# A squared-ReLU MLP on Trainium2: in the last quarter, two of the eight outputs over all tokens and six in two passes by token half

## The chip, the core and the metric

The kernel is one program on one core of a Trainium2 chip. The metric is the device time of one execution in microseconds (us), as a median over runs. The engines are called PE (TensorE, with PEld for its weight loads), DVE (VectorE), ACT (ScalarE), POOL (GpSimd) and SP (SyncE, which issues the loads). Each of them works through its own instructions in the order in which the program lists them, and waits where an operand or a buffer isn't ready.

## What is computed

Two layers run over 512 tokens, 256 of context and 256 latent, with 1024 features. Layer 0 mixes tokens by a convolution module, layer 1 by a bidirectional mLSTM, and each layer is followed by an MLP. What matters here is the end of layer 0 and the first product of layer 1:

```
h  = layer_norm(ALPHA * h + g2 * (square(relu(u @ w1)) @ w2))   # layer 0, latent and context rows
u' = h * (1 + scale) + shift                                    # modulation for layer 1
z  = u'[latent] @ up_z                                          # layer 1, latent rows only
xm = u' @ up_x                                                  # layer 1, all rows
```

The hidden width of the MLP is 4096. The layer norm goes over the 1024 features of a token, so it can be finished for a token only when all eight blocks of 128 features are there.

## The kernel before

**Layout.** Features lie on the 128 partitions and tokens on the free dimension: columns 0 to 255 are context (`LO`, s = 0), 256 to 511 latent (`HI`, s = 1). The residual stream is eight tiles x of 128x512. An fp32 product is made of three matmuls (`mm3`, lines 181, 184, 185): the weight is split into a rounded part wh and a rest wl, the activation likewise, and wh·hi, wh·lo and wl·hi are added in PSUM. For each weight block of 128x1024 `split_w` has ACT cast wh (line 150) and DVE subtract for wl (line 151). One output (128 features) over 1024 inputs takes 8 x 3 = 24 matmuls.

**The MLP.** `mlp` (line 1040) takes the hidden width in four quarters c. A quarter makes eight hidden tiles hid (`e1`) and then adds its share to the eight x tiles (`e2`, whose line 1071 is a DVE instruction per output and token half). For c < 3 the second product is a `gemm` over all 512 tokens. For c = 3 it is `gemm2` (line 284): pass 1 makes all eight outputs for the latent half, pass 2 all eight for the context half, each matmul 256 columns wide. The order of pass 2 is the list `AGAIN`, 4 5 6 7 0 1 2 3 (line 1109).

**Buffers.** Split weights go round a ring of four (`NW`); a slot comes free when its last matmul has read it. `gemm2` keeps outputs 0 to 3 in the ring over both passes, and 4 to 7 in tiles u (`keep`). Raw weights go round a ring of three, loaded by SP.

**The norm.** In the last quarter `feed0` (line 1111) hands each finished half tile to a `Norm` (line 487). With the fourth tile of a half it has a sum, whose mean is made on PE (line 507) and copied by ACT (508); with the fifth, all tiles so far are shifted on DVE (523), squared on ACT (525, 528), and sums and squares are collected on DVE (529, 531, 533). After the eighth, `finish` (line 536) takes PE matmuls (543), small DVE and ACT steps (545 to 553) and PE transposes (556). Then `u1_half` (line 1125) applies it, tile by tile: two DVE instructions (561, 562), two on ACT for hi and a full-precision copy S (584), one on DVE for lo (585).

**Order around the change.** The latent half is finished first, since `up_z` (line 1156) reads only latent columns. `feed0` advances `u1_half(1)` by two tiles at each output of pass 2, and `u1_half(0)` goes along with the outputs of `up_z`. `up_z` begins with three outputs side by side (`ko=3`). The order within an engine isn't written by hand: a scheduler lists each engine's instructions when the program is built.

Of the kernel before, what the change touches and what calls it, by code (L numbers as in the profile page):

```python
# [71 lines left out]
def hybrid_kernel(ctx: ExitStack, tc: tile.TileContext, xT, vecs_d, wdw_d, ada0_w, ada_w, wg_d, pw1a, pw1, pw2, w1_0, w2_0,  # L72
# [18 lines left out]
    def tmp(tag, dt=F32):  # L91
        return tp.tile([P, T], dt, tag=tag, name=nm(tag), bufs={"E": 4, "S": 2, "L": 2, "F": 1}[tag])
# [56 lines left out]
    def split(hi, lo, src):  # L149
        c = nc.scalar.copy(hi, src)  # L150
        lastsub[0] = nc.vector.tensor_tensor(lo, src, hi.bitcast(F32), op=ALU.subtract).ins  # L151
        return c.ins
# [68 lines left out]
    def gemm(*a, **k):  # L221
        for _ in gemm_steps(*a, **k):
            pass
# [60 lines left out]
    def gemm2(*a, **k):  # L284
        for _ in gemm2_steps(*a, **k):
            pass
# [180 lines left out]
    def comb(l, gname, bname, sc, sh, streams=(0, 1)):  # L467

        ca = con.tile([P, 2, DT], F32, name=nm("ca"))
        cb = con.tile([P, 2, DT], F32, name=nm("cb"))  # L470
        for s in streams:
            nc.vector.scalar_tensor_tensor(ca[:, s, :], ad(l, s, sc), 1.0, VA(gname), op0=ALU.add, op1=ALU.mult)
            nc.vector.scalar_tensor_tensor(cb[:, s, :], ad(l, s, sc), 1.0, VA(bname), op0=ALU.add, op1=ALU.mult)
            nc.vector.tensor_tensor(cb[:, s, :], cb[:, s, :], ad(l, s, sh), op=ALU.add)
        return ca, cb
# [8 lines left out]
    HALVES = [(0, LO), (1, HI)]  # L484


    class Norm:
# [22 lines left out]
        def feed(self, t):  # L510

            self.ts.append(t)
            if len(self.ts) <= 4:
                self.add(t)
                return
            if len(self.ts) == 5:
                self.mean()
            for x_ in self.ts[self.i:]:
                self.shift(x_)
# [520 lines left out]
    def mlp(w1, w2, uu, res, n, g2, feed, hmake, after, each1=None, each=None, keep=None, pre=None):  # L1040

        def part(c):
            hid = {}

            def e1(m, ps, s=None, sl=slice(0, n)):
                r, q = tmp("E")[:, :ps.shape[-1]], tmp("E")[:, :ps.shape[-1]]
                nc.scalar.activation(r, ps, AF.Relu)
                nc.vector.tensor_tensor(q, r, r, op=ALU.mult)
                if m not in hid:
                    if n == T:  # L1050
                        hid[m] = hmake(F32R), hmake(F32R)
                    else:
                        t = hmake(F32R)
                        hid[m] = t[:, :n], t[:, n:2 * n]
                split(hid[m][0][:, sl], hid[m][1][:, sl], q)
                if each1:
                    each1(c, m, s)

            groups = range(4 * c, 4 * c + 4)
            if keep and c == 0:  # L1060
                gemm2(w1, groups[:3], uu, HALVES, e1, keep, ko=3)
                gemm(w1, groups[3:], uu, n, lambda m, ps: e1(m + 6, ps))
            else:
                gemm(w1, groups, uu, n, e1, ko=0 if c else 3 + Z.pre4 if pre else 3, pre=pre if c == 0 else None)
            after(c)

            def e2(m, ps, s=None, sl=slice(0, n)):
                for s_, g, sl_ in g2:
                    if s is None or s == s_:
                        p_ = ps if s is not None else ps[:, sl_]  # L1070
                        nc.vector.scalar_tensor_tensor(res[m][:, sl_], p_, g[:, m:m + 1], res[m][:, sl_],
                                                       op0=ALU.mult, op1=ALU.add)
                if c == 3:
                    feed(m, s)
                if each:
                    each(c, m, s)

            hs = [hid[i] for i in range(8)]
            if keep and c == 3:
                gemm2(w2[c], range(4), hs, HALVES[::-1], e2, keep, again=AGAIN)  # L1080
            else:
                gemm(w2[c], range(4), hs, n, e2, ko=Z.kw2)

        for c in range(4):
            part(c)
# [9 lines left out]
    def each1(c, m, s):  # L1095
        if c == 0 and uside:
            for _ in range(Z.nu2):
                next(uside[0], None)
        if c in (1, 2) or (c == 3 and m < 2):
            ada_n1.step()  # L1100
# [5 lines left out]
    lns = norm_pair(maker(hp, "ln", 3))  # L1106
    cab1, u1, sides = [], {}, []

    AGAIN = [4, 5, 6, 7, 0, 1, 2, 3]

    def feed0(m, s):
        sl = HALVES[s][1]
        lns[s].feed(x[m][:, sl])
        if len(lns[s].ts) == DT:
            lns[s].finish()
            if not cab1:
                ada_n1.flush()
                cab1.extend(comb(1, "ln2_g0", "ln2_b0", "sc1", "sh1"))
            if s == 1:
                sides.append(u1_half(s))  # L1120
        if s == 0 and sides:
            for _ in range(2):
                next(sides[0], None)

    def u1_half(s):
        for i in range(DT):
            f = i if s else AGAIN[i]
            xn = lns[s].apply(i)
            if s:
                u1[f] = U(F32R), U(F32R)  # L1130
            affine_half(*[t[:, HALVES[s][1]] for t in u1[f]], xn, s, *cab1, f)
            yield

    mlp(w1_0, w2_0, uu, x, T, [(s, ad(0, s, "g2"), sl) for s, sl in HALVES], feed0, HD, after0, each1, each0, keep=U)


# [849 lines left out]
```

## Time and profile before

| | |
|---|---|
| median of 3 runs | 1671.9 us (1670.12 to 1672.25) |
| the profiled execution | 1670.06 us |
| its span, first to last instruction | 1668.3 us |
| PE busy | 1656.0 us, 8920 matmuls |
| DVE busy | 1030.2 us |
| ACT busy | 742.2 us |
| mean granted PE clock | 0.998 |

The profile is of one execution. A timeline row gives the start in us from the span's start, the duration, the engine, the line and the operation, then written and read tiles; idle time ahead of it stands in brackets with what ended it. Matmuls overlap in their pipeline, so the distance between two starts tells their cost, not the duration. The same holds in part for DVE and ACT: consecutive instructions start a little before the one ahead has ended. A row of the stages gives the length of a stretch, the busy time of each engine with its instructions, the granted clock, and the share and rate of the DMA engines.

### The profile page before, as it was taken

How to read it: one execution, taken by the hardware profiler on the slowest of the kernel's cores; microseconds unless marked ns; L12 is line 12 of the kernel's file. 1: busy time of each engine (PE TensorE's matmuls, PEld its weight loads, DVE VectorE, ACT ScalarE, POOL GpSimd, SP SyncE). 2: the span in 40 equal slices, each digit the busy share in tenths (PEclk: the TensorE clock that was granted, in tenths of full speed). 3: DMA queues.
4: the chain of work that ended last, by engine and by line, in shares of the span. 5: the costliest groups of instructions: out<-in, count | busy, mean ns of one | idle time of the engine just before them, and what ended most of it. 6: DMA issues, size and time to landing. Idle time of an engine off the chain costs nothing.

```text
span 1668.3 us, 22876 instructions
## 1 busy us (share of the span) xinstructions
PE 1656.0 (99%) x8920; PEld 1364.9 (82%) x8920; DVE 1030.2 (62%) x1857; ACT 742.2 (44%) x1196; POOL 14.3 (1%) x64
## 2 busy tenths in 40 slices
PE   9999999999999999999999999999999999999998
PEld 6665898888888998877788899888878888878887
DVE  6555895666635765761143663564389876786677
ACT  4313573232324476652243532442368654655453
POOL 0000000000000000000000000000000000000001
PEclk9999999999999999999999999999999999999999
DMA  9565223444324064556775743455375556675552
GB/s 359 201 216 208 85 75 114 151 145 136 136 101 152 10 233 160 185 194 251 266 259 174 259 171 120 143 198 175 130 246 190 192 213 213 253 274 190 179 186 92
DMA packets 73901, 301.63 MB, mean 181 GB/s; under 512 B 7518, under 2 KB 23682, under 8 KB 43968
## 3 DMA queue, kind: packets, MB, share of 16 engines
q1 hardware_dynamic: 56080, 285.44, 48.3%
q10 hardware_dynamic: 17712, 14.72, 2.6%
q8 instruction: 70, 1.15, 0.3%
q14 instruction: 39, 0.32, 0.1%
HBM read 284.37 MB, written 15.77 MB: 180 GB/s over the span
## 4 chain that ended last, share of the span: by engine, by line
PE 96%; DVE 2%; DMA 1%; issue 0%; ACT 0%; SPq 0%; ACTq 0%; DVEq 0%
PE mm L181 17%; PE mm L184 17%; PE mm L185 17%; PE mm L196 7%; PE mm L212 4%; PE mm L214 4%; PE mm L213 4%; PE mm L197 4%; PE cv L212 2%; PE cv L214 2%; PE cv L213 2%; PE fl L343 1%; PE ln L181 1%; PE cv L839 1%; PE ln L184 1%; PE ln L185 1%
## 5 line engine op out<-in xcount | busy, mean ns | idle before, releaser
L151 DVE TENSOR_TENSOR wl<-raw,wh 128x1024 fp32r<-128x1024 f32 x344 | 418.9, 1222 | 276.2 <-ACT wh L150 263.5
L150 ACT CAST wh<-raw 128x1024 fp32r<-128x1024 f32 x344 | 358.7, 1051 | 502.3 <-PE mm L184 278.3
L184 PE MATMUL mm<-u,wh 128*128 128x512 f32 (+1 forms) x808 | 291.6, 361 | 0.2 <-DVE u L594 0.2
L181 PE MATMUL mm<-u,wh 128*128 128x512 f32 (+1 forms) x680 | 243.6, 359 | 0.0
L185 PE MATMUL mm<-u,wl 128*128 128x512 f32 (+1 forms) x680 | 241.3, 355 | 0.0
L184 PEld LDWEIGHTS mm<-u,wh 128*128 128x128 f32 x808 | 152.6, 189 | 22.2 <-DVE u L594 0.5
L181 PEld LDWEIGHTS mm<-u,wh 128*128 128x128 f32 x680 | 128.4, 189 | 25.2 <-issue 5.9
L185 PEld LDWEIGHTS mm<-u,wl 128*128 128x128 f32 x680 | 128.4, 189 | 18.6 <-issue 0.8
L212 PE MATMUL mm<-wh,xl 128*128 128x512 f32 x256 | 101.0, 395 | 0.1
L181 PE MATMUL mm<-xm,wh 128*128 128x512 f32 x256 | 101.0, 394 | 0.0
L213 PE MATMUL mm<-wh,xl 128*128 128x512 f32 x256 | 100.0, 391 | 0.0
L185 PE MATMUL mm<-xm,wl 128*128 128x512 f32 x256 | 99.7, 390 | 0.0
L214 PE MATMUL mm<-wl,xl 128*128 128x512 f32 x256 | 99.2, 391 | 0.0
L181 PE MATMUL mm<-hid,wh 128*128 128x512 f32 (+1 forms) x256 | 93.3, 364 | 0.0
L185 PE MATMUL mm<-hid,wl 128*128 128x512 f32 (+1 forms) x256 | 92.8, 363 | 0.0
L184 PE MATMUL mm<-hid,wh 128*128 128x512 f32 (+1 forms) x256 | 92.8, 363 | 0.0
L196 PE MATMUL mm<-x,wh 128*128 128x512 f32 x232 | 81.1, 398 | 0.0
L426 DVE SCALAR_TENSOR_TENSOR S<-ar,cs,S 128x512 f32<-128x512 f32 x56 | 40.8, 749 | 59.4 <-DMA ar<-ada_w 59.2
L184 PE MATMUL mm<-qq,wh 128*128 128x272 f32 x256 | 73.9, 289 | 0.0
L181 PE MATMUL mm<-qq,wh 128*128 128x272 f32 x256 | 73.5, 288 | 0.0
L185 PE MATMUL mm<-qq,wl 128*128 128x272 f32 x256 | 73.5, 288 | 0.0
L196 PE MATMUL mm<-u,wh 128*128 128x512 f32 x192 | 68.7, 399 | 0.0
(535 smaller groups left out, 3253.2 us busy)
## 6 DMA issues: line engine op xcount, KB each, us to landing
raw<-w SPq DMA_DIRECT2D x64, 1024.0 KB, 4.8
raw<-wo SPq DMA_DIRECT2D x32, 1024.0 KB, 4.8
raw<-ada_w SPq DMA_DIRECT2D x22, 1024.0 KB, 6.5
ar<-ada_w SPq DMA_DIRECT2D x80, 256.0 KB, 3.7
raw<-wv SPq DMA_DIRECT2D x16, 1024.0 KB, 6.8
raw<-wqT SPq DMA_DIRECT2D x16, 1024.0 KB, 6.2
raw<-wq SPq DMA_DIRECT2D x16, 1024.0 KB, 4.9
raw<-wk SPq DMA_DIRECT2D x16, 1024.0 KB, 5.1
```

Of the source, the lines that this page charges most:

```text
L150: c = nc.scalar.copy(hi, src)
L151: lastsub[0] = nc.vector.tensor_tensor(lo, src, hi.bitcast(F32), op=ALU.subtract).ins
L181: a = nc.tensor.matmul(ps, wh, xh, start=start, stop=False)
L184: nc.tensor.matmul(ps, wh, xl, start=False, stop=False)
L185: lastmm[0] = nc.tensor.matmul(ps, wl, xh, start=False, stop=stop).ins
L196: todo = [lambda s_, e_: nc.tensor.matmul(ps, wh, r[0], start=s_, stop=e_), lambda s_, e_: nc.tensor.matmul(ps[:, :n], wl, r[0][:, :n], st ...
L197: lambda s_, e_: nc.tensor.matmul(ps[:, :n], wl, r[0][:, :n], start=s_, stop=e_)]
L212: nc.tensor.matmul(ps, xh, wh, start=start, stop=False)
L213: nc.tensor.matmul(ps, xl, wh, start=False, stop=False)
L214: nc.tensor.matmul(ps, xh, wl, start=False, stop=stop)
L343: a = mark_unit[0] = nc.tensor.matmul(ps[32 * j:32 * j + 32], cs[:, kt, 14 - 2 * v:46 - 2 * v], blocks[kt], start=first and kt < 4, stop=l ...
L426: nc.vector.scalar_tensor_tensor(a, w, c, a, op0=ALU.mult, op1=ALU.add)
```

## The change

For c = 3 the second product is now a `gemm` of the first group (outputs 0 and 1, all 512 tokens) and then a `gemm2` of the other three groups: six outputs for the latent half, then six for the context half, in the order 6 7 2 3 4 5. Outputs 0 and 1 feed the norms of both halves at once (`s is None`). `AGAIN` is now the order in which context tiles reach their norm, and is used by `u1_half(0)`.

```diff
             if keep and c == 3:
-                gemm2(w2[c], range(4), hs, HALVES[::-1], e2, keep, again=AGAIN)
+                gemm(w2[c], range(1), hs, n, e2)
+                gemm2(w2[c], range(1, 4), hs, HALVES[::-1], lambda m, *r: e2(m + 2, *r), keep, again=[4, 5, 0, 1, 2, 3])
             else:
                 gemm(w2[c], range(4), hs, n, e2, ko=Z.kw2)
...
-    AGAIN = [4, 5, 6, 7, 0, 1, 2, 3]
+    AGAIN = [0, 1, 6, 7, 2, 3, 4, 5]

     def feed0(m, s):
+        if s is None:
+            feed0(m, 1)
+            feed0(m, 0)
+            return
         sl = HALVES[s][1]
         lns[s].feed(x[m][:, sl])
```

Pass 2 ends with the four outputs whose weights lie in the ring, before and after. Lines of the changed kernel are one higher from line 1081 on and five higher from about line 1112 on; the helpers' lines are the same. The scheduler lists the instructions around the hand-over to `up_z` anew, at three places.

On PE, the end of pass 2 and the start of `up_z`. Before, these rows stand there (mm_5193 is the last output of pass 2, mm_5270 and mm_5275 are the first two of `up_z`; the u on the left of a pair are hi and lo of the latent u'):

```order
L185 MATMUL mm_5193<-hid_4569,wl_4672 128x256
L181 MATMUL mm_5270<-u_4941,wh_5266 128x256
L184 MATMUL mm_5270<-u_4942,wh_5266 128x256
L185 MATMUL mm_5270<-u_4941,wl_5267 128x256
L181 MATMUL mm_5275<-u_4941,wh_5271 128x256
L184 MATMUL mm_5275<-u_4942,wh_5271 128x256
L185 MATMUL mm_5275<-u_4941,wl_5272 128x256
```

Now it is these, with mm_5135 the last output of pass 2, and mm_5212, mm_5217, mm_5224 and cv_5316 the first four outputs of `up_z`:

```order
L185 MATMUL mm_5135<-hid_4569,wl_4761 128x256
L181 MATMUL mm_5212<-u_4937,wh_5208 128x256
L184 MATMUL mm_5212<-u_4938,wh_5208 128x256
L181 MATMUL mm_5217<-u_4937,wh_5213 128x256
L184 MATMUL mm_5217<-u_4938,wh_5213 128x256
L181 MATMUL cv_5316<-u_4937,wh_5297 128x256
L184 MATMUL cv_5316<-u_4938,wh_5297 128x256
L181 MATMUL mm_5224<-u_4937,wh_5220 128x256
L184 MATMUL mm_5224<-u_4938,wh_5220 128x256
L185 MATMUL mm_5212<-u_4937,wl_5209 128x256
```

The first wl is read by the ninth matmul of `up_z` where it was the third, and a matmul of the fourth output, with its wh, stands among the first eight.

On DVE, the last two outputs of pass 2 (lines 1071 of x_213 and x_259) and what stands around them. Before, the wl of the first `up_z` output (wl_5267) is some rows above this piece, and the last of `u1_half(1)` (line 585) above that:

```order
L1071 SCALAR_TENSOR_TENSOR x_213<-mm_5162,ada_97,x_213 128x256
L151 TENSOR_TENSOR wl_5272<-raw_5264,wh_5271 128x1024
L523 TENSOR_TENSOR x_213<-x_213,ln_2181 128x256
L151 TENSOR_TENSOR wl_5279<-raw_5276,wh_5278 128x1024
L529 TENSOR_TENSOR ln_2182<-ln_2182,L_5189 128x256
L533 TENSOR_TENSOR ln_2180<-ln_2180,x_213 128x256
L1071 SCALAR_TENSOR_TENSOR x_259<-mm_5193,ada_97,x_259 128x256
L151 TENSOR_TENSOR wl_5356<-raw_5276,wh_5355 128x1024
```

Now, with the last two outputs x_305 and x_351:

```order
L1071 SCALAR_TENSOR_TENSOR x_305<-mm_5104,ada_97,x_305 128x256
L562 TENSOR_TENSOR x_443<-x_443,ln_4889 128x256
L585 TENSOR_TENSOR u_5091<-S_5092,u_5090 128x256
L523 TENSOR_TENSOR x_305<-x_305,ln_2181 128x256
L1071 SCALAR_TENSOR_TENSOR x_351<-mm_5135,ada_97,x_351 128x256
L533 TENSOR_TENSOR ln_2180<-ln_2180,x_305 128x256
L523 TENSOR_TENSOR x_351<-x_351,ln_2181 128x256
L151 TENSOR_TENSOR wl_5209<-raw_5206,wh_5208 128x1024
L585 TENSOR_TENSOR u_5099<-S_5100,u_5098 128x256
```

The first wl of `up_z` has moved from ahead of the last two outputs to behind the last one, and the last lo of the latent half (u_5099) stands behind it.

On ACT, the casts of the four wh of `up_z`, of which now the last two (wh_5220, wh_5297) stand as follows, each waiting for the ring slot of one of the last two outputs of pass 2:

```order
L150 CAST wh_5220<-raw_5218 128x1024
L584 ACTIVATE u_5090<-x_397,cb_4901,ca_4900 128x256
L584 ACTIVATE S_5092<-x_397,cb_4901,ca_4900 128x256
L150 CAST wh_5297<-raw_5218 128x1024
L584 ACTIVATE u_5098<-x_443,cb_4901,ca_4900 128x256
L584 ACTIVATE S_5100<-x_443,cb_4901,ca_4900 128x256
```

The last two tiles of the latent half now stand behind these casts; before, all sixteen of these ACT instructions stood ahead of the first cast.

## The prediction

> **What bounds the kernel now.** I read the page first, then the stages around the change, then the timelines of PE, DVE and ACT there.
>
> ```profile
> PE 1656.0 (99%) x8920; PEld 1364.9 (82%) x8920; DVE 1030.2 (62%) x1857; ACT 742.2 (44%) x1196; POOL 14.3 (1%) x64
> PE 96%; DVE 2%; DMA 1%; issue 0%; ACT 0%; SPq 0%; ACTq 0%; DVEq 0%
> ```
>
> PE is busy 99% of the span and holds 96% of the chain that ended last. So the change can win only PE time, and it loses whatever PE is made to wait. The other engines matter where their work has to be ready for PE. The stages are pass 1, pass 2, the first three outputs of `up_z`, and the next two and a half:
>
> ```profile
> core 0: us, PE busy (x) PEld busy (x) DVE busy (x) ACT busy (x) POOL busy (x), PEclk, DMA share, GB/s
> 533.00:556.73 23.73, 23.73 (x195) 23.47 (x195) 13.27 (x29) 5.30 (x11) 0.00 (x0) 1.00 0.24 90
> 556.73:582.19 25.46, 25.46 (x212) 25.20 (x211) 22.59 (x66) 14.92 (x29) 0.00 (x0) 1.00 0.00 1
> 582.19:592.20 10.01, 10.01 (x86) 9.92 (x85) 7.57 (x21) 3.69 (x8) 0.80 (x9) 1.00 0.59 211
> ```
>
> In pass 2 DVE is busy for 22.59 of 25.46 us: beside PE's matmuls it normalizes the latent half for `up_z`, and PE doesn't wait at all. That is the cover which the change shortens. DMA is idle there (1 GB/s), so loads play no part.
>
> **PE's own time.** The rows give the cost of a matmul by the distance between starts, and the marks of the passes:
>
> ```profile
> 499.73 0.39 PE L181 MATMUL mm<-u,wh 128*128 128x512 f32 x1
> 505.17 0.39 PE L181 MATMUL mm<-u,wh 128*128 128x512 f32 x1
> ...
> 533.05 0.28 PE L181 MATMUL mm<-hid,wh 128*128 128x256 f32 x1
> ...
> 536.41 0.28 PE L184 MATMUL mm<-hid,wh 128*128 128x256 f32 x1
> 536.64 0.38 PE L181 MATMUL mm<-hid,wh 128*128 128x256 f32 x1
> ...
> 556.73 0.60 PE L451 MATMUL mm<-ident,F 128*128 128x128 f32 x4
> ...
> 582.19 0.28 PE L181 MATMUL mm<-u,wh 128*128 128x256 f32 x1
> ...
> 585.07 0.28 PE L181 MATMUL mm<-u,wh 128*128 128x256 f32 x1
> ```
>
> From 499.73 to 505.17 lie 24 matmuls of 512 columns, one output: 5.44 us. From 582.19 to 585.07 lie 24 of 256 columns: 2.88 us. Two halves cost 5.76, a whole output 5.44, so two outputs save **0.64 us**. The Trainium skill ("TensorE: Matmul & The Clock Gate", the section "Wait — 56ns, not 53.3ns?") gives a warm matmul N columns at 2.4 GHz plus about 2.5 ns; by that estimate the 48 pairs save 48 x 2.5 ns = 0.12 us. The rows show a fixed part of about 13 ns (2 x 120 - 227), and I keep them.
>
> The gap at 536.41 to 536.64 is a wait for the last hidden tile, whose lo DVE ends late:
>
> ```profile
> 536.62 0.69 DVE L151 TENSOR_TENSOR hid<-E,hid 128x512 fp32r<-128x512 f32 x1 [0.69 <-ACT hid L150]
> ```
>
> The lo is there at 537.31. The first output now needs it at its 22nd matmul, 533.05 + 21 x 0.227 = 537.8, so this wait goes: about 0.25 us with the reshuffled matmuls around it.
>
> Pass 1 now ends at 533.05 + 2 x 5.44 + 6 x 2.88 + 0.4 (the mean's matmul) = 561.6, where it was 556.73: 4.9 us **later**. Pass 2 has two outputs less: 25.46 - 5.76 = 19.7 us, so it ends at 561.6 + 19.7 = 581.3, where it was 582.19: **0.9 us earlier**. Without any wait the kernel would gain 0.9 us.
>
> **The normalization of the latent half.** It starts 4.9 us later, and PE wants it 0.9 us earlier. Had it 5.8 us to spare? DVE's rows:
>
> ```profile
> 561.70 0.42 DVE L561 TENSOR_TENSOR x<-x,ln 128x256 f32<-128x256 f32 x1 [0.55 <-PE ln L556]
> ...
> 571.18 0.42 DVE L585 TENSOR_TENSOR u<-S,u 128x256 fp32r<-128x256 f32 x1
> 571.52 0.42 DVE L503 TENSOR_TENSOR ln<-ln,x 128x256 f32<-128x256 f32 x1
> ...
> 573.95 0.43 DVE L585 TENSOR_TENSOR u<-S,u 128x256 fp32r<-128x256 f32 x1
> 574.29 0.42 DVE L523 TENSOR_TENSOR x<-x,ln 128x256 f32<-128x256 f32 x1
> ...
> 583.51 0.47 DVE L1071 SCALAR_TENSOR_TENSOR x<-mm,ada,x 128x256 f32<-128x256 f32 x1
> 583.91 1.21 DVE L151 TENSOR_TENSOR wl<-raw,wh 128x1024 fp32r<-128x1024 f32 x1
> 585.04 0.41 DVE L523 TENSOR_TENSOR x<-x,ln 128x256 f32<-128x256 f32 x1
> ```
>
> A short instruction of 256 columns takes 0.335 us of the queue (571.18 to 571.52), an L1071 0.40, a wl 1.14. Before, the last lo of the latent half began at 573.95, 8.2 us ahead of PE's first need at 582.19. That alone would bear a shift of 5.8. But DVE isn't free in between: from 574.29 it shifted the context tiles and made the wl of `up_z`. The context half now has its fifth tile at the third output of pass 2 instead of the fifth. Therefore its shifts are listed between the latent tiles, and the first wl comes behind all of this.
>
> I walk the new list of DVE from its first L561 to the first wl of `up_z`. The start is 561.70 + 4.9 = 566.6. The list has 40 short instructions (40 x 0.335 = 13.4 us), six L1071 (2.4 us) and the wl itself (1.2 us, to its end): 17.0 us, hence 583.6 without a wait. Before, from 561.70 to 574.29, 27 short ones and five L1071 make 11.05 us of 12.59: 1.5 us were waits (for PE, for ACT's S, for the instruction just ahead). I take 1.0 us here, since the added shifts stand where DVE waited; with 1.5 x 17.0 / 12.6 = 2.0 it would be more.
>
> - **Taken:** the wl ends at 584.6.
> - **Lower bound:** the wl stands behind the L1071 of the last output, which can't begin before pass 2 ends. 581.3 + 0.1 + 0.40 + 2 x 0.335 + 1.2 = 583.7.
> - **Upper bound:** 585.6.
>
> PE reads that wl in its ninth matmul of `up_z`. The eighth is done at 581.3 + 8 x 0.12 = 582.25; among them, the matmul with the fourth wh waits a little, and inside the same wait. The cast's price is in these rows of ACT:
>
> ```profile
> 576.51 1.05 ACT L150 CAST wh<-raw 128x1024 fp32r<-128x1024 f32 x1 [0.47 <-PE mm L184]
> ...
> 572.82 0.60 ACT L584 ACTIVATE u<-x,cb,ca 128x256 fp32r<-128x256 f32 x1 [0.36 <-DVE x L562]
> 573.32 0.59 ACT L584 ACTIVATE S<-x,cb,ca 128x256 f32<-128x256 f32 x1
> ```
>
> The fourth wh is ready at about 581.35 + 1.05 = 582.4. Behind it on ACT are the hi and the S of the last latent tile (0.50 and 0.59 us): 583.5, and its lo on DVE is behind the wl. No matmul needs them within the next 0.9 us. So PE waits **2.3 us** (1.4 to 3.3), at one place.
>
> Later waits in `up_z`: the matmuls L543 need the last sums, four short DVE instructions behind the wl, at 584.6 + 4 x 0.335 = 585.9. PE reaches them at 584.6 + 9 x 0.12 = 585.7. The second wl follows at 587.1, when PE is at about 587.8. I take nothing for these (0 to 0.7).
>
> **The sum:** -0.9 + 2.3 = **+1.4 us** (bounds +0.5 and +3.1). Against the profiled execution's 1670.06 us, which is its span of 1668.3 and 1.8 around it, this is 1671.5. The median of the runs shown, 1671.9, is 1.8 above that execution, and I forecast on the median: 1673.3. All of it is below 0.2% (3.3 us), about what a measurement of this kernel can tell from no change.
>
> **Rivals.**
>
> *The wait is made up later: not slower.* If a later stage waits for a load whatever PE does, PE may arrive late there at no cost. The chain has one long piece of that kind:
>
> ```profile
> 821.43 9.05 DMA raw<-wv
> ```
>
> If this load started by itself, the 2.3 us would vanish in it and the gain of 0.9 be left: 1671.0. It decides from the point where the load is issued by a free queue and not by a freed buffer. Against it speaks that the chain reaches it through ACT and DVE instructions that follow PE. Chance 0.12.
>
> *The backlog walks on: clearly slower.* The context norm starts later as well, and the wl of the sixth output of `up_z` had no slack:
>
> ```profile
> 596.84 1.23 DVE L151 TENSOR_TENSOR wl<-raw,wh 128x1024 fp32r<-128x1024 f32 x1
> ...
> 598.23 0.28 PE L185 MATMUL mm<-u,wl 128*128 128x256 f32 x1
> ```
>
> It ended at 598.07 and was read at 598.23. By the walk the same point is late by 1.3 us on DVE and on PE alike, so nothing is added. If DVE's waits are at the upper bound and each small step of `finish` queues behind a wl (three wl now stand among them, 3 x 1.14 = 3.4 us), about 3 us are added, and PE loses 1.4 + 3 = 4.4: 1676.3. Chance 0.25.
>
> *The granted clock falls behind the wait: slower.* A wait of 2.3 us might throttle PE; at half clock for as long as the wait itself lasted, PE would lose 2.3 us more: 1675.6. This row speaks against it:
>
> ```profile
> 0.00:20.00 20.00, 17.95 (x143) 13.79 (x143) 11.17 (x51) 10.00 (x20) 2.52 (x13) 1.00 0.93 366
> ```
>
> Here PE was idle for 2.05 us and the clock is 1.00. The Trainium skill ("TensorE: Matmul & The Clock Gate", Part 1, on the HAM clock gate) says that the clock halves after an idle window of about 3.4 us; by that rule a wait of 2.3 us stays below it, and the trace agrees as far as it goes. Chance 0.07.
>
> *A wait that I don't see goes, and the kernel is faster by over 0.2%.* The passes hold no PE wait but the gap shown, so 3.3 us can't be found there. Chance 0.03.
>
> **How the numbers follow.** The forecast, +0.5 to +3.1 us, has 0.53; with the wait that is made up later, 0.65 lie within 0.2%. Slower by over 0.2% are the backlog and the clock, 0.32; faster 0.03. The range goes from the made-up case on a median as low as the lowest run (1670.12 - 0.9 = 1669.2) to the backlog on the highest run and a little more (1672.25 + 4.4 = 1676.7; I take 1677.5, since that case has no upper bound).
>
> **What would show it.** In the profile of the changed kernel, pass 1 ends at about 561.6 and `up_z` starts at about 581.3. PE then has one gap of 1.4 to 3.3 us behind eight matmuls, ended by the wl of DVE line 151, and that wl starts right behind the L523 of the last context tile. DVE is busy nearly without a break from 566 to 586. From 600 us on all PE rows are later by the same 1 to 2 us. If the gap is missing, or the first wl ends before 583.7, the walk is wrong. If further gaps stand at L543, L556 or the sixth output, the backlog rival is right; if the granted clock is below 1 behind the gap, the clock is.

## The result, and the profile after

The change is slower: **1675.63 us** in the median of 18 executions (1672.97 to 1679.55), where the kernel before has 1670.47 (18 executions, 1669.46 to 1672.25). The ratio is 1.0027 with a 95% interval of 1.0021 to 1.0034. The forecast, 1673.3, lay 2.3 us too low, inside its range. The difference itself was missed by more: +1.4 us was forecast (bounds +0.5 and +3.1), +5.2 measured between the two medians. The spread is a finding of its own: before's executions lie within 2.8 us, those of the change within 6.6.

The profiled execution of the changed kernel is the longest of its 18, 1679.55 us. Its page and its stages (columns as in the stages above: length, busy time of each engine, granted clock, DMA share, GB/s):

```profile
span 1677.2 us, 22767 instructions
PE 1662.2 (99%) x8872; PEld 1367.7 (82%) x8872; DVE 1027.7 (61%) x1855; ACT 741.6 (44%) x1194; POOL 14.3 (1%) x64
```

```profile
535.40:563.98 28.58, 28.58 (x196) 26.64 (x194) 16.57 (x34) 7.39 (x13) 0.00 (x0) 1.00 0.30 112
563.98:583.67 19.69, 19.69 (x164) 19.45 (x163) 17.35 (x57) 12.93 (x26) 0.00 (x0) 1.00 0.01 1
583.67:594.19 10.52, 8.59 (x45) 8.18 (x44) 8.47 (x19) 3.12 (x7) 0.79 (x9) 0.68 0.30 100
```

PE has 48 matmuls fewer, as it should, and is busy 6 us longer. Pass 1 begins 2.35 us later than before (535.40 against 533.05), for a reason that lies 470 us ahead of the change and comes last below; from there the two passes take 28.58 + 19.69 = 48.27 us, before 49.14 (533.05 to 582.19). So the passes gain 0.87 us. The third row is where it goes wrong: PE waits for 1.9 of 10.5 us and its clock is 0.68 in the mean. The rows of PE there, with each wait in brackets:

```profile
584.03 0.28 PE L184 MATMUL mm<-u,wh 128*128 128x256 f32 x1
584.94 0.38 PE L181 MATMUL cv<-u,wh 128*128 128x256 f32 x1 [0.63 <-ACT wh L150]
...
585.42 0.28 PE L184 MATMUL mm<-u,wh 128*128 128x256 f32 x1
587.00 0.39 PE L185 MATMUL mm<-u,wl 128*128 128x256 f32 x1 [1.30 <-DVE wl L151]
```

By the distances of the starts less 0.12 for a matmul, the two gaps cost 0.79 + 1.46 = 2.25 us. What ends the second one is the first wl of `up_z`, in DVE's rows:

```profile
568.94 0.42 DVE L561 TENSOR_TENSOR x<-x,ln 128x256 f32<-128x256 f32 x1 [0.55 <-PE ln L556]
...
585.39 0.42 DVE L523 TENSOR_TENSOR x<-x,ln 128x256 f32<-128x256 f32 x1
585.72 1.22 DVE L151 TENSOR_TENSOR wl<-raw,wh 128x1024 fp32r<-128x1024 f32 x1
```

It stands right behind the shift of the last context tile and ends at 586.94. And then the clock, in stretches of 3.41 us:

```profile
580.53:583.95 3.42, 3.42 (x31) 3.42 (x30) 3.34 (x10) 3.42 (x8) 0.00 (x0) 1.00 0.00 0
583.95:587.36 3.41, 1.48 (x11) 1.07 (x10) 3.38 (x8) 2.54 (x6) 0.00 (x0) 1.00 0.00 0
587.36:590.77 3.41, 3.41 (x19) 3.41 (x18) 2.06 (x4) 0.00 (x0) 0.00 (x0) 0.50 0.26 34
590.77:594.19 3.42, 3.42 (x17) 3.42 (x18) 2.83 (x7) 0.30 (x1) 0.79 (x9) 0.50 0.66 273
594.19:597.60 3.41, 3.41 (x31) 3.41 (x31) 0.56 (x3) 0.00 (x0) 0.00 (x0) 1.00 0.90 286
```

The edges are those at which the granted clock changes. PE is idle for 1.93 of the 3.41 us up to 587.36; the next two stretches run at exactly half clock, with 19 and 17 matmuls where a full one has 31. That costs 12 + 14 matmuls of 0.12 us, 3.1 us, more than the wait itself.

A third loss lies 620 us further on, where the code wasn't touched. Three rows of the changed kernel, from the timelines of DVE and PE, then the first of these instructions in DVE's timeline of before:

```profile
1216.68 1.29 DVE L461 TENSOR_TENSOR G<-mm,G 128x512 f32<-128x512 f32 x2 [1.28 <-DMA G<-rows_d]
...
1217.43 0.50 PE L212 MATMUL mm<-wh,xl 128*128 128x512 f32 x1 [0.81 <-DVE G L461]
...
1221.63 0.50 PE L214 MATMUL mm<-wl,xl 128*128 128x512 f32 x1 [0.29 <-DVE wl L151]
```

```profile
1208.74 1.28 DVE L461 TENSOR_TENSOR G<-mm,G 128x512 f32<-128x512 f32 x2
```

DVE waits 1.28 us for the load of G, and PE then waits for DVE, 0.81 and 0.29 us: 1.1 us together on PE. Before there is no wait.

### The profile page after: what moved, and what is told of

The parts are those of the page before. It is cut to its first block, busy times and chain, and to the rows that moved or that the text cites. A ratio compares the mean times of both kernels' runs of the same rounds, so it can differ in the third digit from the quotient of the medians.

```text
span 1677.2 us, 22767 instructions
## 1 busy us (share of the span) xinstructions
PE 1662.2 (99%) x8872; PEld 1367.7 (82%) x8872; DVE 1027.7 (61%) x1855; ACT 741.6 (44%) x1194; POOL 14.3 (1%) x64
## 5 line engine op out<-in xcount | busy, mean ns | idle before, releaser
L181 PE MATMUL mm<-hid,wh 128*128 128x512 f32 (+1 forms) x272 | 99.6, 366 | 0.0
L185 PE MATMUL mm<-hid,wl 128*128 128x512 f32 (+1 forms) x272 | 99.0, 364 | 0.0
L184 PE MATMUL mm<-hid,wh 128*128 128x512 f32 (+1 forms) x272 | 99.0, 364 | 0.0
```

The costliest lines, as they stand in the source:

```text
L181: a = nc.tensor.matmul(ps, wh, xh, start=start, stop=False)
L184: nc.tensor.matmul(ps, wh, xl, start=False, stop=False)
L185: lastmm[0] = nc.tensor.matmul(ps, wl, xh, start=False, stop=stop).ins
```

## The experiments

Each was timed in turn with the kernel before on the same chip; ratios carry their 95% intervals. Three theories went in. **W**: the PE wait comes from the order on DVE alone. **C**: with two outputs fewer behind it, the work of DVE and ACT for `up_z` has no room, in whatever order. **K**: the clock falls because of the wait. A fourth, **F**, came out of the traces: the late G is due to where a transfer of instructions falls.

**e1: the context half's norm is fed later.** The first two outputs go to the latent norm alone, and their context halves are fed at the end of pass 2 (with `AGAIN` in that order).

```diff
-            feed0(m, 0)
...
+        if s == 0 and m == 5:
+            for k in (0, 1):
+                lns[0].feed(x[k][:, sl])
```

> The change, but the context half of outputs 0 and 1 is handed to its norm behind the other six context tiles instead of at once; the order of the tiles in that norm follows. Theory W (the wait at the hand-over comes from context shifts that the early feed puts ahead of the first wl of up_z on DVE): the first wl stands early again, the gap of PE behind the eighth matmul of up_z goes, and the time is 0.9 us under before (ratio 0.9995). Rival C (the cover is too short for DVE's work in whatever order): the first wl is early, but what has to be ready next, the sums for L543 and the second wl, stands behind the same shifts; by the walk on DVE it ends about 20.5 us behind the first L561 and PE waits 1 to 2 us there, so the time is 0.1 to 1.1 us above before, and more in executions whose granted clock falls behind that wait.

Measured: 1673.26 (1671.94 to 1677.74), before 1670.59; ratio 1.0018 (1.0009 to 1.0027). PE's two waits at its hand-over, in the timeline:

```profile
586.20 0.38 PE L181 MATMUL cv<-u,wh 128*128 128x256 f32 x1 [0.78 <-ACT wh L150]
...
587.50 0.39 PE L185 MATMUL mm<-u,wl 128*128 128x256 f32 x1 [0.46 <-DVE wl L151]
```

The stretches of 3.41 us in which they lie and that follow them:

```profile
585.60:589.01 3.41, 2.35 (x19) 2.27 (x20) 3.41 (x8) 2.96 (x5) 0.44 (x9) 1.00 0.19 19
589.01:592.43 3.42, 3.42 (x19) 3.42 (x18) 2.72 (x6) 1.83 (x3) 0.35 (x1) 0.50 0.90 353
```

The first wl came early, but the wait moved to a later cast and a later wl and was not gone: 1.24 where the change has 1.93. One stretch at half clock follows, where the change has two. The time lies 2.7 us above before, outside both forecasts; neither had the late G, which e1 has as well (table below). This order removes a third of the wait and can't decide between W and C.

**e2: the change, with the wait filled.** Twelve products that nothing reads stand between the last output of pass 2 and `up_z`.

```diff
+                def e2_(m, ps, s, sl):
+                    if s == 0 and m == 3:
+                        pin[0] = True
+                        idle(psum("fl"), 12)
+                        pin[0] = False
+                    e2(m + 2, ps, s, sl)
...
```

> The change, with twelve matmuls of 128 columns on a constant tile (their result is not read) between the last output of pass 2 and up_z, about 2.1 us of PE work where PE waits for about 2.1 us. Theory K (part of the loss, about 3 us in some executions, is the granted clock, which falls because PE is idle at the hand-over): the clock stays at 1.00 in the stretch, the executions lie together, and the time is that of the best executions of the change, 2 to 3 us above before (ratio 1.0012 to 1.0018), although no wait was removed. Rival N (the clock falls for a reason that has nothing to do with the wait, or the filler costs as much as it saves): the times spread from 2.5 to 7 us above before as with the change, or are higher by up to 2 us.

Measured: 1672.25 (1671.54 to 1674.15); ratio 1.0010 (1.0001 to 1.0019). The 20 us around the hand-over:

```profile
580.00:600.00 20.00, 20.00 (x172) 19.95 (x170) 17.91 (x41) 11.06 (x20) 0.79 (x9) 1.00 0.35 129
```

The clock stays at 1.00. The program does more on PE than the change, has no less to do elsewhere, and is 3.4 us faster in the median. Not all of that is the clock's: G is on time in this program's trace (table below), which by the change's trace is worth 1.1 us of it. That also explains why it lies a little below the 2 to 3 us over before that were forecast. The clock of every execution decides: of the change's 18, nine have a mean granted clock of 0.998 or 0.999 and take 1672.97 to 1675.61 us, the other nine have 0.996 or 0.997 and take 1675.66 to 1679.55. One stretch of 3.41 us at half clock lowers the mean by 0.001. All eleven of e2 have 0.998 or 0.999. K is shown: the fall of the clock hangs on PE standing still.

**e3: four outputs over all tokens instead of two.**

```diff
-                gemm(w2[c], range(1), hs, n, e2)
-                gemm2(w2[c], range(1, 4), hs, HALVES[::-1], lambda m, *r: e2(m + 2, *r), keep, again=[4, 5, 0, 1, 2, 3])
+                gemm(w2[c], range(2), hs, n, e2)
+                gemm2(w2[c], range(2, 4), hs, HALVES[::-1], lambda m, *r: e2(m + 4, *r), keep)
...
-    AGAIN = [0, 1, 6, 7, 2, 3, 4, 5]
+    AGAIN = [0, 1, 2, 3, 4, 5, 6, 7]
```

> The same change with four outputs over all tokens and four in two passes. PE saves 1.5 us of its own (4 x 0.32 and the 0.25 of the hidden tile). The latent norm starts 10 us later than before and pass 2 is 13.9 us long. Theory W and rival C agree on the direction: the walk on DVE (39 short instructions, four L1071, a wl, 17.2 us with waits) puts the first wl at about 588.9 where PE arrives at 581.6, a wait of about 7 us, so 5.8 us above before, and about 3 us more where the clock falls (ratio 1.0035 to 1.0053). If instead the wait does not depend on the cover, it stays at 2 us and the time is 0.5 us above before.

Measured: 1679.4 (1679.03 to 1679.88); ratio 1.0050 (1.0037 to 1.0064). The stretches of its hand-over:

```profile
582.10:585.51 3.41, 0.73 (x4) 0.44 (x4) 3.08 (x10) 2.96 (x7) 0.00 (x0) 1.00 0.00 0
585.51:588.92 3.41, 1.87 (x8) 1.78 (x8) 1.78 (x9) 1.38 (x4) 0.79 (x9) 0.50 0.00 0
588.92:592.34 3.42, 2.20 (x10) 2.21 (x11) 3.42 (x8) 1.62 (x4) 0.00 (x0) 0.50 0.00 0
592.34:595.75 3.41, 3.41 (x18) 3.41 (x18) 3.37 (x6) 0.31 (x1) 0.00 (x0) 0.50 0.69 262
```

More of the same change gives more waits (idle 2.7, 1.5 and 1.2 us in three stretches) and three stretches at half clock, each right behind one in which PE stood still. PE's own saving grows as the working says (pass 1's start to `up_z` is 47.6 us, 1.5 less than before), and drowns.

**e4: the context half's norm gives way, by 150 steps of priority.**

```diff
-        lns[s].feed(x[m][:, sl])
+        with tc.high_priority(-150) if s == 0 else nullcontext():
+            lns[s].feed(x[m][:, sl])
+            if len(lns[s].ts) == DT:
+                lns[s].finish()
         if len(lns[s].ts) == DT:
-            lns[s].finish()
             if not cab1:
```

> The change, with a lower priority in the scheduler for the context norm of this stage only, so that on DVE the latent tiles and the first four wl of up_z stand ahead of the context shifts, and PE's list starts up_z with its matmuls in the old order. Theory W: the gap at the hand-over goes (at most 0.5 us left), the clock stays at 1.00, and PE's own saving is left: 0.4 to 0.9 us under before (ratio 0.9995 to 0.9998). Rival C: DVE's work still doesn't fit, PE waits at least 1.5 us at the latent tiles or the wl, and the time is at least 0.6 us above before.

Measured: 1673.76 (1672.02 to 1675.38); ratio 1.0017 (1.0008 to 1.0025). PE has no wait at the hand-over, and then these, 26 us later in its timeline:

```profile
609.57 0.39 PE L181 MATMUL mm<-u,wh 128*128 128x256 f32 x1 [0.25 <-ACT wh L150]
...
611.50 0.39 PE L185 MATMUL mm<-u,wl 128*128 128x256 f32 x1 [1.43 <-DVE wl L151]
```

ACT's timeline has these rows 10 us ahead of them:

```profile
599.80 1.28 ACT L550 ACT_TABLE_LOAD   x1
...
601.41 1.28 ACT L1159 ACT_TABLE_LOAD   x1
```

W's forecast missed. C's came true by its letter (1.7 us of waits at a wh and a wl, 3.2 us above before), but the waits stand 26 us behind the place that C is about. The norm had given way so far that its square root (line 550) fell among the silus of `up_z` (line 1159): two table loads of 1.28 us on ACT that the change doesn't have there. Eight instructions of the context tiles follow them (line 584, 604.52 to 608.48), and the cast that PE waits for stands behind these. The loads alone are not shown to be the cause: e1 has the same pair 10 us earlier (588.59 and 591.75) and no PE wait behind it, though PE was at half clock there until 592.43. So the lateness of the norm counts too, and the run doesn't decide between W and C. G is late here as well.

**e5: the same, by 60 steps.** Two wl go ahead, and the norm stays ahead of the first silu. The edit is e4's with -60.

> The change, with the context half's norm work at a priority 60 steps behind its place (150 in the run before): on VectorE the first two weight rests of up_z stand ahead of it, the other six behind or between, and the norm's square root stays ahead of the first silu, so no second table load. Theory W (only the order on VectorE made the wait, and the last try paid for the late norm, not for lost cover): no TensorE wait over 0.3 us from 575 to 620 us, granted clock 1.00 there, time 0.5 to 0.9 us under before: 1669.5 to 1670.2. Theory C (with two outputs fewer there is not enough time for the work of VectorE and ScalarE, in whatever order): waits of 1 to 2 us in sum turn up at another place between 585 and 615 us, the clock dips behind them in some executions, 1671.5 to 1674.

Measured: **1671.16** (1670.55 to 1673.61), before 1670.79; ratio 1.0003 (0.9994 to 1.0011). The stretches of 20 us at the hand-over and behind it:

```profile
580.00:600.00 20.00, 19.95 (x167) 19.70 (x166) 17.15 (x41) 14.07 (x27) 0.79 (x9) 1.00 0.40 136
600.00:620.00 20.00, 20.00 (x169) 20.00 (x169) 14.16 (x22) 16.24 (x27) 0.00 (x0) 1.00 0.76 245
```

PE idles for 0.05 us in 40, at full clock. C falls: the same work fits behind six outputs without a wait. W holds as far as order is the cause; the edit moves the norm's instructions on ACT as well as on DVE, so that it is DVE's order alone is not shown. But the time is neither the 1669.5 to 1670.2 that W gave nor the 1671.5 to 1674 of C: it is the same as before's. In the trace PE runs 0.8 to 1.2 us ahead of before from 590 to 1205 us, and loses it here, in DVE's timeline:

```profile
1209.04 1.29 DVE L461 TENSOR_TENSOR G<-mm,G 128x512 f32<-128x512 f32 x2 [1.25 <-DMA G<-rows_d]
```

**e8: before, with the same 60 steps**, as a control.

> The kernel before with the same 60 steps of lower priority for the context half's norm, without the change: a control for the run with the change. Three weight rests stand ahead of the norm's shifts; before has no wait there, so W and C both expect 0: 1670.2 to 1671.2, clock 1.00. If it gains 0.3 us or more, what the priority does has nothing to do with the change.

Measured: 1670.68 (1670.13 to 1672.21); ratio 1.0000 (0.9991 to 1.0009). The priority by itself does nothing.

**e6: before, with a wait made at the hand-over.** Only the first wl of `up_z` is listed behind the norm's last sum.

```diff
-        lastsub[0] = nc.vector.tensor_tensor(lo, src, hi.bitcast(F32), op=ALU.subtract).ins
+        with tc.issue_after(behind.pop()) if behind else nullcontext():
+            lastsub[0] = nc.vector.tensor_tensor(lo, src, hi.bitcast(F32), op=ALU.subtract).ins
...
-                nc.vector.tensor_tensor(self.acc, self.acc, t, op=ALU.add)
+                added[0] = nc.vector.tensor_tensor(self.acc, self.acc, t, op=ALU.add).ins
...
+                    if keep and s == 0 and m == 3:
+                        behind.append(added[0])
```

> The kernel before, without the change: only the first weight rest (wl) of up_z is issued behind the last accumulation of the context half's norm on VectorE. From the last product of the first MLP it then takes 0.40 + 2 x 0.335 + 1.22 = 2.3 us until that rest is there, TensorE has 8 products of 0.12 us in that time, so waits of 1.4 to 2.2 us with what follows. Theory K (the granted clock falls behind a TensorE wait of that size, whatever makes it): clock 0.50 for 3.4 or 6.8 us right behind the wait, 1.7 to 3.4 us on top, 1673.5 to 1676.2, and a spread of over 2 us among the executions. Rival (the fall belongs to something else in the change): clock 1.00 throughout, 1672.0 to 1672.8.

Measured: 1672.81 (1671.0 to 1674.78); ratio 1.0011 (1.0002 to 1.0019). The wait became smaller than planned, since the scheduler put other matmuls of `up_z` into it. PE's timeline:

```profile
583.13 0.36 PE L184 MATMUL mm<-u,wh 128*128 128x256 f32 x1 [0.19 <-DVE x L1074]
...
585.09 0.39 PE L188 MATMUL mm<-u,wl 128*128 128x256 f32 x1 [0.47 <-DVE wl L152]
```

The stretches around them:

```profile
582.65:586.06 3.41, 2.68 (x19) 2.17 (x18) 3.34 (x6) 1.19 (x2) 0.00 (x0) 1.00 0.00 0
586.06:589.47 3.41, 3.41 (x17) 3.41 (x18) 3.05 (x7) 0.30 (x1) 0.79 (x9) 0.50 0.52 156
```

Without the change, one stretch at half clock follows a wait of 0.7 us in brackets (19 matmuls in 3.41 us). The fall belongs to the wait and not to the change. The median lies below the 1673.5 to 1676.2 that K gave, because the wait was smaller than the 1.4 to 2.2 us expected. By its time alone the run would suit the rival as well; it is the clock of 0.50 behind the wait that decides.

**e7: the same with twelve idle products.** The edit is e2's, on top of e6.

> The run with the wait alone, with 12 idle products (2.6 us) that nothing reads between the last product of the first MLP and the first of up_z. Theory K: the clock stays at 1.00, the time is before + 2.6 and what is left of the wait (0 to 0.5): 1673.0 to 1673.8, with a spread under 2 us; so more idle products than the wait needs cost no more than the wait with the clock's fall. Rival (products that fill the wait don't matter): the same fall as in the run without them, 1674.5 or more.

Measured: 1673.88 (1673.04 to 1674.84); ratio 1.0018 (1.0010 to 1.0027). Its 20 us around the hand-over:

```profile
580.00:600.00 20.00, 20.00 (x172) 20.00 (x171) 16.69 (x38) 10.23 (x18) 0.79 (x9) 1.00 0.32 125
```

The clock stays at 1.00 and the spread is 1.8 us, where e6 has 3.8: K's mechanism holds. The median is 1.1 us above e6's. That isn't the price of the fill alone: at 1422 us PE waits 0.75 us for a cast that waited 2.09 us for a load of wo, and e6 has no wait there. Whether a fill is worth it for a wait as short as e6's is therefore not shown.

**The late load.** The traces of all these programs can be laid side by side at the load of G. Its issue and the queues are the same in each (a load of wo 2.88 us ahead, bo 0.38 us behind). What differs is one transfer of 16 KB, marked "instruction", on a queue of its own (q8). The queues of the changed kernel in the 5 us from G's issue (packets, MB, share of the 16 engines):

```profile
q1 hardware_dynamic: 367, 1.35, 85.0%
q8 instruction: 1, 0.02, 1.3%
```

Before has this in the 5 us from its own issue of G, and no second queue:

```profile
q1 hardware_dynamic: 375, 1.37, 89.9%
```

| program | 16 KB transfer of instructions, from G's issue | last packet of G, from its issue | DVE waits for G |
|---|---|---|---|
| the change | +2.15 us | 4.88 us | 1.28 us |
| e1 | +1.80 | 4.93 | 1.33 |
| e4 | +1.86 | 4.58 | 0.98 |
| e5 | +1.61 | 4.86 | 1.25 |
| before, e2, e3, e6, e7, e8 | none from -6 to +8 | 3.16 to 3.28 | 0 |

A transfer of 8 KB on another instruction queue follows G's issue by 6.4 to 8.2 us in all of them, when G has landed. In the four with the wait, 7 to 10 of G's 128 packets are late, about one sixteenth, which would be the share of one of the 16 DMA engines; the trace doesn't say which engine carried a packet. From G's issue to the end these four take 465.2 to 465.9 us; before, e2, e6 and e8 take 463.4 to 464.1. (e3 and e7, with G on time, take 465.4 and 465.0, with another PE wait of 0.8 us behind it.) There are 70 such transfers in the changed program, and a program of another length has them at other places. The runs that follow move the transfer by way of the idle products at the program's very start.

**e9: e5 with 24 PE instructions fewer at the start.**

```diff
-    ones = con.tile([P, P], F32, name="ones")
+    ones2 = con.tile([P, 2 * P], F32, name="ones2")
+    ones = ones2[:, 0:P]
...
-    idle(spare, 13)
+    for _ in range(6):
+        nc.tensor.matmul(spare[:, 0:2 * P], ones, ones2, start=True, stop=True)
+    idle(spare, 1)
```

> The change with the norm's priority 60 steps back, and at the program's start 6 idle products of 256 columns and 1 of 128 in place of 13 of 128: the same 5.4 us of idle work in 24 TensorE instructions fewer. Theory F (the 1.1 us that the change loses near 1210 us come from a 16 KB transfer of instructions that falls between the issue of G<-rows_d and its landing; the program's length decides where it falls; 48 more instructions moved it 8 us, so 24 fewer move it some 4 us, behind the landing): VectorE no longer waits for G, no TensorE wait at L212, end 0.9 us ahead of before in the trace, time 1.0 us less than without it: 1669.6 to 1670.3. Rival (G lands late for another reason, in every program with the change): the waits of 0.8 and 0.3 us stay, 1670.9 to 1671.5.

Measured: 1674.48 (1672.47 to 1677.79); ratio 1.0023 (1.0014 to 1.0032): slower, where F had said faster. Yet what F says of G came true: the transfer moved to 4.46 us behind G's issue, G's last packet landed at 3.43 us, and DVE didn't wait for it. The transfer now met the next load, of wo, which took 7.6 us from issue to landing where before's takes 5.4, and ACT's cast waited for that one, 4.07 us where the control e10 has 1.93. ACT's timeline:

```profile
1215.56 2.00 ACT L151 CAST wh<-raw 128x1024 fp32r<-128x1024 f32 x2 [4.07 <-DMA raw<-wo]
```

PE's timeline, 10 us on:

```profile
1225.93 0.76 PE L1407 MATMUL ln<-E,tri 128*128 128x128 f32 x2 [2.34 <-DVE E L1393]
```

Through DVE's chain the delay had reached PE, as 2.34 us in one piece, and two stretches at half clock followed (1226.00 to 1232.83). So a wait brings the clock down 640 us away too.

**e10: before with the same idle products**, the control.

> The kernel before with the same 6 + 1 idle products at the start: a control. Its transfer of instructions lay 10 us ahead of G's issue and moves some 4 us towards it, still ahead. F: no wait near 1205 to 1212 us, 1670.2 to 1671.2. If the wider idle products themselves gain 0.5 us or more, the gain of the run with the change is not F's.

Measured: 1671.04 (1670.14 to 1671.63); ratio 1.0000 (0.9991 to 1.0008), as forecast. The wider idle products change nothing by themselves.

**e11: the change with them.**

> The change as it is, with the 6 + 1 idle products at the start. F: the wait for G and the 0.8 and 0.3 us at L212 and L214 are gone, the waits and the clock at the hand-over stay as they were: about 1 us less than the change in its median, 1674.0 to 1675.0, and the fastest executions at 1671.7 to 1672.2 where the change had 1672.97. Rival: waits near 1210 us and times as with the change.

Measured: 1676.65 (1673.63 to 1680.33); ratio 1.0033 (1.0022 to 1.0045). As in e9: G is on time (3.26 us), the transfer at +4.26 meets the load of wo, and PE waits 1.20 us at 1227 us, this time with the clock at 1.00 behind it. The forecast missed for the same reason.

**e12: e5 with 32 PE instructions more at the start**, so that the transfer falls ahead of the loads.

```diff
-    idle(spare, 13)
+    for n_ in (5, 4, 4, 4):
+        for _ in range(n_):
+            nc.tensor.matmul(spare[:, 0:1], ones, ones[:, 0:1], start=True, stop=True)
+        idle(spare, 1)
```

> The change with the norm's priority 60 steps back, and at the program's start 17 idle products of 1 column and 4 of 128 in place of 13 of 128: about the same 5.4 us in 32 TensorE instructions more. Theory F: the 16 KB transfer of instructions moves 4 to 6 us ahead, to 2 to 5 us before the issue of G, where no product waits for the transfers in flight; G lands within 3.4 us of its issue, no wait for it on VectorE, no TensorE wait over 0.5 us from 1200 to 1230 us, clock 1.00: the end 0.6 to 1.2 us ahead of before, 1669.5 to 1670.2. Rival (the loss near 1210 us stays with every program that has the change, wherever the transfer falls): 1671 or more, with a wait there that F does not explain. If the short idle products lower the clock in the first 15 us, the program starts 1 us or more late, and the mark near 1210 us alone decides.

Measured: 1677.01 (1674.63 to 1678.26; five executions); ratio 1.0037 (1.0024 to 1.0051). The start was late, by much more than 1 us: the first 16 matmuls of line 343 take 1.94 us here and 1.07 in before (that row stands in the next section), as they would at a lower clock, and pass 1 begins at 538.50 where e5 has 532.94. So the mark decides, as was said. Two rows of PE's timeline in e12:

```profile
10.38 1.94 PE L343 MATMUL fl<-raw,cs 128*32 128x256 f32 x16
...
538.50 0.39 PE L181 MATMUL mm<-hid,wh 128*128 128x512 f32 x1
```

The start of pass 1 in e5:

```profile
532.94 0.39 PE L181 MATMUL mm<-hid,wh 128*128 128x512 f32 x1
```

And G in DVE's timeline of e12, with no bracket behind it:

```profile
1213.46 1.27 DVE L461 TENSOR_TENSOR G<-mm,G 128x512 f32<-128x512 f32 x2
```

The transfer fell 4.60 us ahead of G's issue, and G's last packet landed 3.21 us behind it. PE has no wait from 1200 to 1230 us. From G's issue to the end e12 takes 463.6 us, as before does, and e5 465.2. From the start of pass 1 to the end e12 takes 1673.0 - 538.5 = 1134.5 us, e5 1668.9 - 532.94 = 1136.0, before 1668.3 - 533.05 = 1135.25. With the transfer out of the way the change is 0.75 us ahead of before at the end, about what PE saves. That figure rests on one trace of each: the controls e8 and e10, which have no change either, take 1135.9 and 1135.2. That G is late where the transfer falls in its way, and on time where it falls ahead or behind, is shown for the profiled executions. A gain in the time of the kernel is not: e12's median is nearly 7 us above before's. Why three of e12's five executions take 2 to 3 us longer than the profiled one (1674.96; the shortest is 1674.63) stays open.

No version beats both kernels. The best with the change, e5, is as fast as before (1.0003).

## Why the prediction was right and where not

**The time: in its range by luck.** The forecast stood on 1671.9, the median of three runs; 18 runs give 1670.47. With +5.2 in place of +1.4, the time lies in the range because that base was 1.4 us too high and because the range reached up to 1677.5 for another rival, the backlog, which didn't happen.

**PE's saving: right.** -0.9 forecast, -0.87 in the passes, and about -0.75 at the end once nothing else is in the way (e12).

**The marks: right.** With the 2.35 us by which this execution is late taken off: pass 1 ends at 561.6 (forecast 561.6), `up_z` starts at 581.3 (581.3), DVE's first L561 at 566.6 (566.6), the first wl ends at 584.6 (584.6). It stands right behind the shift of the last context tile, as said. DVE's rows from 568.94 to 586.94 hold the 40 short instructions and six L1071 of the walk, and its waits come to 18.0 - 17.0 = 1.0 us. That 1.0 was picked between nothing and 2.0, so the exact hit is partly luck.

**The PE wait: right in size, not in place.** Forecast 2.3 us in one gap behind eight matmuls; measured 2.25 by the starts, in two gaps, the first 0.8 us for the fourth wh. The working had that cast "inside the same wait"; PE works through four matmuls between the two.

**"The granted clock falls behind the wait", chance 0.07: this is the step that failed.** The sum put the fall at nothing, and it is the largest part of what was missed. The working priced it at 2.3 us for "as long as the wait itself lasted"; measured are one or two stretches of 3.41 us at half clock, 1.7 us each. Two reasons against it were given, and both fail.

The first was the row of the first 20 us, PE idle for 2.05 and the clock 1.00. That row cannot speak. The same product of 128 columns tells the clock by its own time. Here it is in PE's timeline at the start of before, 26 of them:

```profile
1.12 4.57 PE L175 MATMUL cv<-ones 128*128 128x128 f32 x26 [1.12 <-DVE ones L129]
6.37 1.07 PE L343 MATMUL fl<-raw,cs 128*32 128x256 f32 x16 [0.68 <-DMA raw<-ada_w]
```

And at the hand-over of e7, 24 of them:

```profile
582.62 2.84 PE L178 MATMUL fl<-ones 128*128 128x128 f32 x24
585.29 0.50 PE L546 MATMUL ln<-inv_c,ln 128*128 128x1 f32 x4
```

At the hand-over one takes (585.29 - 582.62) / 24 = 0.111 us. At the start the first 26 take 4.57 us, 0.176 in the mean, so a part of them ran slower, as half clock would have it; the view writes 1.00 there all the same. The record of the granted clock begins at 4.09 us in before's trace, and ahead of its record the view writes 1.00. (An idle product stands as two matmuls in the trace, so 13 are 26 and twelve are 24.)

The second was the Trainium skill ("TensorE: Matmul & The Clock Gate", Part 1, the HAM clock gate): the clock halves after an idle window of about 3.4 us. I read it as an idle time that a wait must reach. The traces agree with the window, and not with that reading. The section also says that the window is 3413 ns long and free-running. The stretches above are 3.41 us, in ones, twos and threes, and each such group begins right behind a stretch in which PE stood still for only a part: 1.93 us (the change), 1.06 (e1), 2.7 (e3), 0.73 (e6). In the change's trace the two falls, at 61.71 and 587.36 us, lie 525.65 us apart, 154 times 3.413. If the windows run freely, an execution's luck decides how a wait is cut by them, and with it how many stretches follow. That fits the spread of the change's executions, and that it shrinks to 2.6 us with the wait filled (e2); the phase was not varied by itself.

**"From 600 us on all PE rows are later by the same": failed.** At 1217 us another 1.1 us are lost in the profiled execution, where a transfer of instructions lies in the way of G's load. The program has 96 PE instructions fewer (48 matmuls, 48 weight loads), and e9 to e12 show that the count moves these transfers. No term of the working and no rival had this. The Trainium skill ("Runtime: NRT & Kernel Launch", "Instruction fetch mechanics") says that instructions come in blocks of 16 KiB on a DMA queue of their own, at a cost mostly hidden; 70 blocks of 256 instructions would be 17,920, and PE alone has 8872 matmuls and as many weight loads, so the 70 are probably PE's. The traces show the block, and that DVE then waits 0.98 to 1.33 us for the load beside it.

**The sum, as measured:** -0.87 + 2.25 + 1.1 = +2.5 us without any fall of the clock: 1670.5 + 2.5 = 1673.0, and the lowest executions are at 1672.97 and 1672.98. One stretch more gives 1674.7, two give 1676.4; the median, 1675.63, lies between. Only one execution of the change has a trace, so that the others have the same waits is assumed. In the profiled execution the parts after pass 1's start come to -0.87 + 2.25 + 3.1 + 1.1 = 5.6 of 6.6 us (1677.2 - 535.40 against 1135.25); of the 1.0 us that is left, 0.5 stand at 1233 us, where PE waits 0.73 for line 1388 of DVE and before waits 0.24 at the same instruction; the rest is not explained.

**The other rivals.** The wait was not made up later: at G's issue, far behind the load of wv, the change is still 1211.28 - 1204.69 - 2.35 = 4.2 us late. The backlog did not walk on: PE has no wait from 587 to 660 us in the change. Its half clock could have hidden one there, but e2, with the same norm and the full clock, has PE busy for all of 20 us. The outcome, slower by over 0.2%, had 0.32, of which 0.25 were for the backlog.

## What to carry to other kernels

A wait of one or two microseconds on a TensorE that is otherwise full is not priced by its length alone: in these runs one or two stretches of 3.4 us at half clock, 1.7 us of loss each, followed most such waits. Look at the clock in stretches of that length behind every one. Where an output is taken from the cover of a hand-over, look first at the order of the engine that feeds it (here 60 steps of priority removed the whole wait), and only then at its load. And a change of under 1 us can be eaten far away by a transfer that merely moved, so compare the traces to the end.

## What the runs showed of the hardware that was not expected

- Half clock behind waits that are far shorter than the window: behind 0.66 us of waits in e6 (1.3 by the starts), behind 1.24 in e1. The 0.81 us at 1217 us in the change did not do it, nor the 1.20 us in e11. So the idle time that the profile shows does not sort them; where the border lies, and why the change's second stretch follows one in which PE was never idle, stays open.
- The 2.35 us at pass 1's start are another such fall. PE waits 0.45 us at 59.62, and the next stretch is at half clock; before has the same code and no fall there. Before isn't free of it either: one of its 24 executions beside e9 to e11 took 1675.97 us at a mean clock of 0.997. The stretches of the changed kernel:

```profile
58.29:61.71 3.42, 2.90 (x10) 1.29 (x10) 2.53 (x3) 2.60 (x5) 0.00 (x0) 1.00 0.23 87
61.71:65.12 3.41, 3.41 (x9) 2.63 (x9) 0.00 (x0) 0.58 (x1) 0.00 (x0) 0.50 0.86 311
```

- A block of instructions on its own queue makes about one sixteenth of a load beside it late; its last packet lands 1.3 to 1.8 us later (4.58 to 4.93 us against 3.16 to 3.28). Nothing in the order of the instructions shows it.
- A square root that slips between silus costs two table loads of 1.28 us on ACT (e4, e1).
